# Side matmuls of all stages put one step behind the elementwise work that feeds them, in fewer and larger steps

## The chip, the cores and the metric

The kernel runs on one core of a Trainium2 chip. The metric is the device time of one execution in microseconds; the times quoted are medians of several runs.

## The reference, cut to what matters

Four layers act on 512 tokens of width 2048, all in float32. Each is a large projection in, a sequence mixer, gates, and a projection out that is added to the residual:

```python
def layer_ab(x, ...):            # 4 heads of gated linear attention (GLA), 8 of forgetting attention
    h = rms_norm(x, norm_g)
    g_q, g_k, g_v, g_lr, g_gate, f_q, f_k, f_v, f_f, f_gate = jnp.split(h @ w_in, split_idx, axis=-1)
    o = gla_chunked(...)                       # chunked recurrence, exp of cumulated decays
    o_fox = forgetting_attention(...)          # causal softmax(q k^T + decay) v
    return x + jnp.concatenate([o_gla, o_fox], axis=-1) @ w_out
def layer_c(x, ...):             # diagonal state-space model (S5), 128 groups of 16 channels
    u, gate = jnp.split(h @ w_in, 2, axis=-1)
    y = s5_ssm(u, ...)                         # x_t = Lbar x_{t-1} + Bbar u_t ; y = Re(C x) + D u
    z = jax.nn.gelu(y); z = z * jax.nn.sigmoid(z @ glu_w + glu_b)
    return x + (z * jax.nn.silu(gate)) @ w_out
def ssd_chunked(x, dt, A, B, C): # in layer D, run twice, beside a convolution of 31 taps and
    ...                                        # two pairs of heads of differential attention
    cb = jnp.einsum("bclgn,bcsgn->bcgls", Cc, Bc)
    y_diag = jnp.einsum("bcgls,bcgjls,bcsgjp->bclgjp", cb, decay_in, xdt)      # inside a chunk of 128
    states = jnp.einsum("bclgn,bcgjl,bclgjp->bcgjpn", Bc, decay_states, xdt)   # then a scan over chunks
    ...
    y_off = jnp.einsum("bclgn,bcgjpn,bcgjl->bclgjp", Cc, prev, jnp.exp(a_cs))  # from the chunks before
```

The order of the program is layer AB, layer C, layer D twice (D0, D1).

## The kernel before, in words

**Projections.** They carry most of the work of TensorE. A float32 product is made of three matmuls on numbers split in a high and a low part (`job_fm`, L244 to L246; `job_tm` and `job_tw` are the same for other layouts), 128x512 outputs in PSUM pool `pp` of 4 buffers. Weights come in units of 512 KB: SP issues the load to `raw` (4 buffers), ScalarE casts the high part (L224), VectorE or, for every fourth unit, GpSimd subtracts it for the low part (L227) into `whl` (3 buffers).

**Side work.** The mixers (GLA, attention, S5, SSD, convolution) and norms are Python generators in two lanes. After each quarter of a job, 24 projection matmuls, `mix()` adds a rate of the table `RATES` to a generator's account and runs one step (up to its next `yield`) for each whole unit; this makes a slot. There are 528 such slots in the program. `pump()` forces steps where a gate needs a result that isn't there yet. So a generator's side matmuls stand on TensorE's queue between projection matmuls, and TensorE works through its queue in order: a side matmul whose operand isn't ready holds up the projection behind it. The Tile framework's scheduler sets the final order from this emission. Side matmuls write to PSUM pool `ax` of 4 buffers; temporaries `t` come from a pool of 8.

```python
    def mix(self):
        for lane in self.lanes:
            if lane:
                m = lane[0]
                m[2] += m[1]
                while m[2] >= 1:
                    m[2] -= 1
                    ...next(m[0])...
```

**Names that follow.** In SSD (`ssd`, L1551), for each of 8 pairs of heads of a layer: the decay matrix is made by four subtract-and-clip instructions for each of the two heads (L1601), an exponential (L1603) and a product (L1604); psD, 8 matmuls of 128x64 tiles (L1617), is the part inside a chunk; psS (L1623) gives the states, which VectorE scans (multiply L1628, add L1630) into S; psO (L1639) multiplies S, one `yield` later. Each of them writes to `ax`. In S5 (`block`, L1189), 16 blocks: 16 matmuls of 64x64 tiles for V (L1202), rotations and scans on VectorE, GpSimd's products, then 4 full matmuls (L1234) and 16 of 64x64 tiles (L1241) for psY. In attention: rope's last sum (L1465), its transposes (L1469), the scores, the softmax, the transposes of p (L843), copied by ScalarE (L845), the products with v; differential attention scales p0 (L1512) before it adds p1. In the convolution branch a tap is L1660. L1565 transposes x for SSD; L190 and L415 sum and spread norms; L1083 and L1113 prepare S5's tables during layer AB; L1435 to L1439 and L855 to L871 are a setup block of tiny instructions for a layer's constants.

Of the kernel before, what the change touches and what calls it, by code (L numbers as in the profile page):

```python
# [9 lines left out]
F32 = mybir.dt.float32  # L10
# [8 lines left out]
D = 2048  # L19
S = 512  # L20
# [4 lines left out]
RATES = {"prep": 1.15, "gla": 2.0, "fox": 2.0, "s5": 4.0, "norm": 1.687, "ssd": 1.27,  # L25
         "att": 1.626, "cfm": 0.827, "dt": 1.0}
# [39 lines left out]
class Kern:  # L66
    def __init__(self, ctx, tc, I, O):
# [20 lines left out]
        self.unit_i = 0  # L88
        self.ahead = {}
# [31 lines left out]
    def small(self, shape, dt=F32, tag=None, bufs=None):  # L121
        tag = tag or f"s{shape[-1]}"
        return self.sm_p.tile(list(shape), dt, tag=tag, name=self.nm(tag),
                              bufs=bufs or (2 if tag in ("gst", "al4", "rm16", "rs16", "rt16", "selr") else 4))
# [70 lines left out]
    def bcast_rows(self, col):  # L195


        nc = self.nc
        ps = self.axp()
# [4 lines left out]
        for i, part in enumerate((hi.bitcast(F32), lo)):  # L204
# [3 lines left out]
            nc.tensor.matmul(ps, self.onesr, dg.rearrange("p c t -> p (c t)"), start=(i == 0), stop=(i == 1))  # L208
        return ps

# [20 lines left out]
    def job_fm(self, W, c0, X, evac, order=(0, 1, 2, 3)):  # L231
# [3 lines left out]
        for qi, kq in enumerate(order):  # L235
# [11 lines left out]
            self.mix()  # L247
        with self.tc.high_priority(offset=2000):
            for m in range(2):
                evac(m, ps[m])  # L250

    def job_tm(self, W, c0, X, evac, order=(0, 1, 2, 3)):
# [3 lines left out]
        for qi, kq in enumerate(order):  # L256
# [13 lines left out]
            self.mix()  # L270
        with self.tc.high_priority(offset=2000):
            for t in range(NC4):
                evac(t, ps[t // 2][:, t % 2, :])
# [18 lines left out]
    def job_tw(self, W, cols, X, evac, order=(0, 1, 2, 3)):  # L292
# [22 lines left out]
        p = parts(6) + parts(7)  # L315
        for t in range(NC4):
# [111 lines left out]
    def rs_pair(self):  # L428

        col = self.rs_columns(self.acc, D)  # L430
        rc = self.par.tile([128, 4], F32, tag="rscol", name=self.nm("rscol"))
        self.nc.vector.tensor_copy(out=rc, in_=col)
        ps = self.bcast_rows(col)
        row = self.par.tile([128, 512], F32, tag="rsrow", name=self.nm("rsrow"))
        self.nc.scalar.copy(out=row, in_=ps)
        return rc, row

# [96 lines left out]
    def layer_ab(self, resid, next_resid, order="to_uj", back=None):  # L534
# [46 lines left out]
        def small_cols():  # L581
# [15 lines left out]
            for q in (32, 64, 96):  # L597
                nc.vector.tensor_tensor(out=sm[0:24], in0=ps[q:q + 24, :], in1=sm[0:24], op=ALU.add)
            sc = self.xo([40, 512])
# [53 lines left out]
        def gla_head(sc, h):  # L653
# [3 lines left out]
            b = la.pop(h)  # L657
            yield
            if h < 3:
                la[h + 1] = gla_la(sc, h + 1)  # L660
                yield
            at = self.mx()
            ps = self.axp()
            for c in range(NC4):
# [4 lines left out]
                                    in1=self.ident.unsqueeze(1).to_broadcast([128, 4, 128]), op=ALU.mult)  # L669
            yield  # L670
            for li, s in enumerate((1, 2, 4, 8, 16, 32, 64)):
                nb = 512 // (2 * s)
                v3 = lambda t: t.rearrange("p (n e) -> p n e", e=2 * s)
                e = self.tmp(tag="t")
                r = v3(b)[:, :, s - 1:s].to_broadcast([128, nb, s])
                nc.vector.tensor_tensor(out=v3(e)[:, :, 0:s], in0=r, in1=v3(b)[:, :, 0:s], op=ALU.subtract)
                nc.vector.tensor_tensor(out=v3(e)[:, :, s:], in0=v3(b)[:, :, s:], in1=r, op=ALU.subtract)
                nc.scalar.activation(out=e, in_=e, func=AF.Exp, scale=1.0 / 16)
                G = e
                nc.vector.tensor_tensor(out=v3(G)[:, :, 0:s], in0=v3(e)[:, :, 0:s], in1=v3(k)[:, :, 0:s],  # L680
                                        op=ALU.mult)
                nc.vector.tensor_tensor(out=v3(G)[:, :, s:], in0=v3(e)[:, :, s:], in1=v3(q)[:, :, s:],
                                        op=ALU.mult)
                odd = lambda t: t.rearrange("p (n e) -> p n e", e=2 * s)[:, :, s:]
                ps = self.axp((128, 256))
                for c in range(NC4):
                    cs = slice(c * 128, (c + 1) * 128)
                    nc.tensor.matmul(ps[:, c * 64:(c + 1) * 64], G[:, cs], odd(G[:, cs]), start=True, stop=True)
                nc.vector.copy_predicated(
                    out=odd(at).rearrange("p (c n) e -> p c n e", c=4),  # L690
                    mask=odd(lev[:, li, :]).unsqueeze(1).to_broadcast([128, 4, 64 // s, s]),
                    data=ps.rearrange("p (c n e) -> p c n e", c=4, e=s))
                yield
            qe = self.tmp(tag="t")
            nc.scalar.activation(out=qe, in_=b, func=AF.Exp, scale=1.0 / 16)
            nc.vector.tensor_tensor(out=qe, in0=qe, in1=q, op=ALU.mult)
# [4 lines left out]
            nc.vector.tensor_tensor(out=ke, in0=ke, in1=k, op=ALU.mult)  # L701
            el = self.small([128, 4], tag="el")
            nc.scalar.activation(out=el, in_=c3(b)[:, :, 127], func=AF.Exp, scale=1.0 / 16)
            yield
# [5 lines left out]
            nc.scalar.copy(out=kt[:, 0:384], in_=ps[:, 0:384])  # L710
            yield
            po = [self.axp(), self.axp()]
            st = None
            for c in range(NC4):
                cs = slice(c * 128, (c + 1) * 128)
                for half in range(2):
                    nc.tensor.matmul(po[half][:, cs], v[c][:, half * 128:(half + 1) * 128], at[:, cs],
                                     start=True, stop=(c == 0))
                    if c > 0:
# [1123 lines left out]
```

## Time and profile before

| | |
|---|---|
| median of 3 runs | 3392.99 us (3390.59 to 3395.67) |
| profiled execution | 3397.99 us |
| its span | 3396.2 us |
| mean granted TensorE clock | 0.992 |
| VectorE, ScalarE, GpSimd busy | 63%, 34%, 30% of the span |

The profiled execution lies 5.0 us over the median. Of its 3397.99 us 1.8 lie outside the span.

### The profile page before, as it was taken

Reading aid. Unit: us, or ns where it says so; the run is one execution under the profiler, and the core shown is the slowest. Engines: PE = TensorE matmul, PEld = TensorE weight load, DVE = VectorE, ACT = ScalarE, POOL = GpSimd, SP = SyncE. Lnnn points to the kernel's source line nnn. Section 1 sums busy time; section 2 is a strip of 40 time slices with the busy share of each in tenths; the row PEclk is TensorE's granted clock in tenths of the full one; section 3 lists DMA queues with packets and bytes.
Section 4 is the critical chain, followed back from the end, with each engine's and each line's share of the span. In section 5 each row is a group of like instructions: output and inputs, shape, how many; then the busy total and the mean of one; then the engine's idle time right before and its main releaser. Section 6 shows DMA issues by size and latency. Waiting matters only on the chain.

```text
span 3396.2 us, 46458 instructions
## 1 busy us (share of the span) xinstructions
PE 3310.2 (97%) x17238; PEld 2710.6 (80%) x17238; DVE 2155.2 (63%) x4409; ACT 1160.3 (34%) x1915; POOL 1007.8 (30%) x993
## 2 busy tenths in 40 slices
PE   8999999999999999999999999988999999998999
PEld 6887887877887777888887878867788787886887
DVE  7765785668347787424257586897526468699632
ACT  4223333334232222323233333324324343323421
POOL 3122414433523333122332121147321212125720
PEclk9999999999999999999999999999999999999999
DMA  6323333344545664434334232333343323233243
GB/s 208 90 71 116 104 106 99 108 122 152 186 129 174 197 209 156 144 120 128 120 108 131 85 87 81 105 104 86 115 139 112 92 83 87 81 112 106 81 134 115
DMA packets 389713, 406.12 MB, mean 120 GB/s; under 512 B 53296, under 2 KB 334774, under 8 KB 389486
## 3 DMA queue, kind: packets, MB, share of 16 engines
q1 hardware_dynamic: 389486, 403.15, 39.3%
q8 instruction: 136, 2.23, 0.3%
q14 instruction: 91, 0.75, 0.1%
HBM read 348.45 MB, written 54.59 MB: 119 GB/s over the span
## 4 chain that ended last, share of the span: by engine, by line
PE 61%; DVE 15%; DMA 3%; issue 2%; POOL 2%; SPq 1%; ACT 1%; DVEq 0%; POOLq 0%; ACTq 0%
PE pp L244 15%; PE pp L246 15%; PE pp L245 15%; PE pp L306 3%; PE pp L305 3%; PE pp L304 3%; DVE mx L1660 2%; DVE whl L227 2%; DVE t L1601 1%; DMA t<-acs 1%; DVE xo L1545 1%; POOL mx L1664 1%; POOL t L1224 1%; DVE ev L517 1%; PE pp L269 1%
## 5 line engine op out<-in xcount | busy, mean ns | idle before, releaser
L246 PE MATMUL pp<-hl,whl 128*128 128x512 f32 x3328 | 1310.5, 394 | 12.1 <-DVE whl L227 9.1
L244 PE MATMUL pp<-hl,whl 128*128 128x512 f32 x3328 | 1314.9, 396 | 3.5 <-ACT hl L328 3.4
L245 PE MATMUL pp<-hl,whl 128*128 128x512 f32 x3328 | 1313.9, 395 | 1.0 <-DVE hl L329 1.0
L224 ACT CAST whl<-raw 128x1024 fp32r<-128x1024 f32 x440 | 461.8, 1050 | 966.3 <-PE pp L246 703.1
L227 DVE TENSOR_TENSOR whl<-raw,whl 128x1024 fp32r<-128x1024 f32 x330 | 428.6, 1299 | 516.7 <-ACT whl L224 510.2
L246 PEld LDWEIGHTS pp<-hl,whl 128*128 128x128 f32 x3328 | 629.4, 189 | 145.9 <-DVE whl L227 10.4
L244 PEld LDWEIGHTS pp<-hl,whl 128*128 128x128 f32 x3328 | 629.5, 189 | 137.5 <-issue 5.8
L245 PEld LDWEIGHTS pp<-hl,whl 128*128 128x128 f32 x3328 | 629.4, 189 | 129.6 <-issue 1.9
L227 POOL TENSOR_TENSOR whl<-raw,whl 128x1024 fp32r<-128x1024 f32 x110 | 277.1, 2519 | 861.8 <-ACT whl L224 776.3
L305 PE MATMUL pp<-whl,hl 128*128 128x512 f32 x704 | 275.6, 392 | 0.0
L306 PE MATMUL pp<-whl,hl 128*128 128x512 f32 x704 | 275.5, 392 | 0.0
L304 PE MATMUL pp<-whl,hl 128*128 128x512 f32 x704 | 273.3, 393 | 0.0
L392 POOL TENSOR_TENSOR t<-t,t 128x512 f32<-128x512 f32 x75 | 111.5, 1498 | 280.0 <-ACT t L385 277.9
L287 ACT CAST whl<-raw 128x1024 fp32r<-128x1024 f32 x88 | 92.3, 1052 | 248.0 <-PE pp L306 187.8
L288 DVE TENSOR_TENSOR whl<-raw,whl 128x1024 fp32r<-128x1024 f32 x66 | 87.1, 1320 | 128.2 <-ACT whl L287 128.1
L1660 DVE SCALAR_TENSOR_TENSOR mx<-xo,col,mx 128x511 f32<-128x511 f32 (+19 forms) x180 | 160.4, 904 | 0.8
L304 PEld LDWEIGHTS pp<-whl,hl 128*128 128x128 f32 x704 | 132.7, 188 | 28.5 <-issue 0.9
L306 PEld LDWEIGHTS pp<-whl,hl 128*128 128x128 f32 x704 | 132.6, 188 | 28.2 <-issue 0.9
L305 PEld LDWEIGHTS pp<-whl,hl 128*128 128x128 f32 x704 | 132.7, 188 | 27.0
L288 POOL TENSOR_TENSOR whl<-raw,whl 128x1024 fp32r<-128x1024 f32 x22 | 53.8, 2446 | 257.9 <-ACT whl L287 245.2
L269 PE MATMUL pp<-whl,hl 128*128 128x256 f32 x384 | 108.2, 285 | 1.0 <-DVE hl L329 1.0
L267 PE MATMUL pp<-whl,hl 128*128 128x256 f32 x384 | 108.6, 285 | 0.5 <-ACT hl L328 0.5
(443 smaller groups left out, 4088.1 us busy)
## 6 DMA issues: line engine op xcount, KB each, us to landing
raw<-w_in SPq DMA_DIRECT2D x160, 512.0 KB
raw<-ab_w_in SPq DMA_DIRECT2D x112, 512.0 KB
raw<-c_w_in SPq DMA_DIRECT2D x64, 512.0 KB
raw<-w_out SPq DMA_DIRECT2D x64, 512.0 KB
raw<-ab_w_out SPq DMA_DIRECT2D x32, 512.0 KB
raw<-glu_w SPq DMA_DIRECT2D x32, 512.0 KB
raw<-c_w_out SPq DMA_DIRECT2D x32, 512.0 KB
raw<-w_in SPq DMA_DIRECT2D x64, 256.0 KB
```

The source lines that it names most:

```text
L224: nc.scalar.copy(out=hl[:, 0, :, :n], in_=raw[:, :, :n])
L227: eng.tensor_tensor(out=hl[:, 1, :, :n], in0=raw[:, :, :n], in1=hl[:, 0, :, :n].bitcast(F32), op=ALU.subtract)
L244: nc.tensor.matmul(ps[m], wh, x[:, 0, :], start=first, stop=False)
L245: nc.tensor.matmul(ps[m], wh, x[:, 1, :], start=False, stop=False)
L246: nc.tensor.matmul(ps[m], wl, x[:, 0, :], start=False, stop=last)
L269: nc.tensor.matmul(o, xl, hl[:, 0, j, :], start=False, stop=last, skip_group_check=True)
L288: (nc.gpsimd if pool else nc.vector).tensor_tensor(out=hl[:, 1], in0=raw, in1=hl[:, 0].bitcast(F32), op=ALU.subtract)
L304: nc.tensor.matmul(ps[t], x[:, 0, ts], hl[:, 0, j, :], start=first and i == 0, stop=False)
L305: nc.tensor.matmul(ps[t], x[:, 0, ts], hl[:, 1, j, :], start=False, stop=False)
L306: nc.tensor.matmul(ps[t], x[:, 1, ts], hl[:, 0, j, :], start=False, stop=last and i == n - 1)
L392: nc.gpsimd.tensor_tensor(out=a, in0=a, in1=sq, op=ALU.add)
L1660: STT(out=Y[i][:, d:], in0=u, scalar=k, in1=Y[i][:, d:], op0=ALU.mult, op1=ALU.add)
```

## The change

It changes when side work is emitted, not what is computed. In every mixer the matmuls of a step now come one step after the elementwise work that makes their operands, and several such groups share a step; the rates are lowered to match, so that generators finish at about the same slots as before (S5's blocks at slot 206 for 196, S5's preparation at 136 for 117, GLA's pairs at 37 and 69 for 35 and 63, the second attention pair of D0 at 322 in both). Steps of a generator fall: GLA's pair 37 to 19, forgetting attention's pair 19 to 11, differential attention's pair 34 to 22, SSD's half 19 to 16, S5 16 blocks of 12 to 139 in all.

Further: forgetting and differential attention are pipelined, with the scores of block n, the transposes of n-1 and the products of n-2 in one step. S5's psY matmuls of block b (64x64 and full) and V of block b+1 are issued together. GLA makes two levels in a step. Rope transposes all its tiles after all its sums. Norms (`rs_pair`, layer D's norms, `ssd_norm`) become generators of two steps, with a flag `rs_ready` that evacuations wait for. ScalarE takes over from VectorE: L1601 (as 128 `Relu`), the convolutions' first taps (L1543 and the 31-tap one) and the layer norm's last scaling; p0's scaling (L1512) falls away, its factor moved into the square and the norm behind it. The number of TensorE matmuls (15670), of DMAs (1406) and the arithmetic of the matmuls stay.

```diff
-RATES = {"prep": 1.15, "gla": 2.0, "fox": 2.0, "s5": 4.0, "norm": 1.687, "ssd": 1.27,
-         "att": 1.626, "cfm": 0.827, "dt": 1.0}
+RATES = {"prep": 0.95, "gla": 0.95, "fox": 1.0, "s5": 2.25, "norm": 1.687, "ssd": 1.05,
+         "att": 1.05, "cfm": 0.827, "dt": 1.0}
...
+            for n in range(len(items) + 2):
+                if n >= 2:
+                    h, qb = items[n - 2]
...
+                    for s in range(qb + 1):
+                        nc.tensor.matmul(po[h][:, qs], vt["f", h][s], t[:, s, :], start=(s == 0), stop=(s == qb))
...
+                if 1 <= n <= len(items):
+                    pt[n - 1] = self.transpose_p(pr.pop(n - 1), items[n - 1][1])
+                if n < len(items):
+                    pr[n] = fox_scores(*items[n], lfhl)
+                yield
...
+                psY = [self.ax.tile([128, 2, 128], F32, tag="ax", name=self.nm("psY")) for _ in range(2)]
                 for h in range(2):
...
+                                nc.tensor.matmul(psY[g][half[i], h, :], w[half[g], 4 + 2 * r + h, half[i]],
+                                                 xs[i][half[g], h, r, :], start=(h + r == 0), stop=False,
+                                                 skip_group_check=True)
+                for g in range(2):
+                    for h in range(2):
+                        nc.tensor.matmul(psY[g][:, h, :], w[:, 8 + 2 * g + h, :], ut[:, g, h, :], start=False,
+                                         stop=True, skip_group_check=True)
+                if b + 1 in us:
+                    cur = inputs(b + 1)
                 yield
...
+            def off_diagonal(i, S, ea):
+                psO = self.axp((128, 384))
+                for c in range(3):
+                    cs = slice(c * 128, (c + 1) * 128)
+                    nc.tensor.matmul(psO[:, cs], S[:, cs], C[:, (c + 1) * 128:(c + 2) * 128], start=True,
+                                     stop=True)
...
-                        TS(out=rb[hh][:, cs], in0=rb[hh][:, cs], scalar1=dac[:, c, 32 + h:33 + h], scalar2=0.0,
-                           op0=ALU.subtract, op1=ALU.min)
-                    nc.scalar.activation(out=rb[hh], in_=rb[hh], func=AF.Exp)
+                        nc.scalar.activation(out=rb[hh][:, cs], in_=rb[hh][:, cs], func=AF.Relu, scale=-1.0,
+                                             bias=dac[:, c, 32 + h:33 + h])
+                    nc.scalar.activation(out=rb[hh], in_=rb[hh], func=AF.Exp, scale=-1.0)
...
+                if prev is not None:
+                    off_diagonal(*prev)
                 psD = self.axp()
```

What this does to the order is seen best on TensorE's queue. In D0's SSD, before, psO's three matmuls of one pair stand one by one between projection matmuls, here the first of them (S is `t_19054`):

```order
L246 MATMUL pp_19526<-hl_16095,whl_19601 128x512
L244 MATMUL pp_19525<-hl_16131,whl_19601 128x512
L1639 MATMUL ax_19076<-xo_17621,t_19054 128x128
L245 MATMUL pp_19525<-hl_16131,whl_19601 128x512
L246 MATMUL pp_19525<-hl_16131,whl_19601 128x512
L244 MATMUL pp_19526<-hl_16131,whl_19601 128x512
```

The same place of the changed kernel (L254 to L256 are the projection, L1748 psO, L1783 psD, L1789 psS, L1738 the transposes of the next x):

```order
L256 MATMUL pp_19161<-hl_15968,whl_19164 128x512
L1748 MATMUL ax_19191<-xo_17610,t_19073 128x128 x3
L1783 MATMUL ax_19197<-t_19059,t_19071 64x128
L1783 MATMUL ax_19197<-t_19060,t_19071 64x128
L1783 MATMUL ax_19197<-t_19059,t_19071 64x128
L1783 MATMUL ax_19197<-t_19060,t_19071 64x128
L1783 MATMUL ax_19197<-t_19059,t_19071 64x128
L1783 MATMUL ax_19197<-t_19060,t_19071 64x128
L1783 MATMUL ax_19197<-t_19059,t_19071 64x128
L1783 MATMUL ax_19197<-t_19060,t_19071 64x128
L1789 MATMUL ax_19206<-t_19150,dx_18734 128x128 x3
L1738 MATMUL ax_19218<-ident,xo_18037 128x128 x4
L254 MATMUL pp_19160<-hl_16009,whl_19234 128x512
```

All 18 stand in one run: psO of the pair before, then psD and psS of this pair. Over the program, between the end of the work on S and a psO matmul (counted from the psS matmul that S comes from) there were 9 projection matmuls at least, mostly 16 to 24; now 24 is the least, which 10 of the 48 psO matmuls have, and 30 of the 48 have 72. For psD the least count is 24 as before, but 96 of 128 rows now have 72. For rope's transposes the least goes from 77 to 120, for psY's from 36 to 56. The p transposes of differential attention had as few as 0 and have 16 at least.

In layer C, TensorE's queue before, where two of S5's 16 psY matmuls stand alone, with the other 14 ten rows on:

```order
L245 MATMUL pp_10728<-hl_9831,whl_10849 128x512
L246 MATMUL pp_10728<-hl_9831,whl_10849 128x512
L1241 MATMUL psY_10841<-t_10782,s5w_10758 64x128
L1241 MATMUL psY_10842<-t_10782,s5w_10758 64x128
L244 MATMUL pp_10727<-hl_9845,whl_10915 128x512
L245 MATMUL pp_10727<-hl_9845,whl_10915 128x512
```

And after, the end of the 16 psY matmuls of a block (L1345), its full ones (L1350) and the first V matmuls of the next block (L1284):

```order
L1345 MATMUL psY_10999<-t_10930,s5w_10782 64x128
L1345 MATMUL psY_10999<-t_10933,s5w_10782 64x128
L1350 MATMUL psY_10998<-mx_10616,s5w_10782 128x128 x2
L1350 MATMUL psY_10999<-mx_10616,s5w_10782 128x128 x2
L1284 MATMUL psV_11024<-mx_10854,s5w_11020 64x128 x2
L1284 MATMUL psV_11025<-mx_10854,s5w_11020 64x128 x2
```

Over the program the runs of side matmuls between projection matmuls go from 399 to 307, those of 64x64 tiles from 70 to 53, those of psD's tiles from 30 to 18.

VectorE's queue in D0's SSD, before: the clips (L1601), the states' scan (L1628, L1630) and the weights' subtraction (L227) in between the taps.

```order
L1601 TENSOR_SCALAR t_19062<-t_19062,dac 128x128 x4
L1660 SCALAR_TENSOR_TENSOR mx_20051<-xo_18971,col_15890,mx_20051 128x508
L1628 TENSOR_TENSOR t_19054<-t_19054,el 128x128
L1601 TENSOR_SCALAR t_19063<-t_19063,dac 128x128 x4
L1660 SCALAR_TENSOR_TENSOR mx_20372<-xo_19355,col_15890,mx_20372 128x508
L1660 SCALAR_TENSOR_TENSOR mx_20051<-xo_18971,col_15890,mx_20051 128x507
L1604 TENSOR_TENSOR t_19062<-t_19062,dx_18724 128x512
L1630 TENSOR_TENSOR t_19054<-t_19054,ax_19050 128x128
L227 TENSOR_TENSOR whl_19754<-raw_19752,whl_19754 128x1024
```

After, the scan (L1796, L1798) with the product of the decays (L1768) and the taps (L1816); no clips are left on this engine.

```order
L1816 SCALAR_TENSOR_TENSOR mx_19597<-xo_18967,col_15818,mx_19597 128x505
L1798 TENSOR_TENSOR t_19225<-t_19225,ax_19206 128x128
L1768 TENSOR_TENSOR t_19211<-t_19211,dx_18728 128x512
L1816 SCALAR_TENSOR_TENSOR mx_19597<-xo_18967,col_15818,mx_19597 128x504
L1796 TENSOR_TENSOR t_19225<-t_19225,el 128x128
L1768 TENSOR_TENSOR t_19212<-t_19212,dx_18728 128x512
L1816 SCALAR_TENSOR_TENSOR mx_19597<-xo_18967,col_15818,mx_19597 128x503
```

VectorE has 4253 instructions for 4411, ScalarE 1955 for 1789. The setup block of D1, which stood late in D0 with one weights' subtraction in its middle, stands there in one piece ahead of the next subtraction.

## Rows read from the trace of the kernel before

**Rows 1.** The page's part 1: engine, busy us, share of the span, instructions.

```profile
PE 3310.2 (97%) x17238; PEld 2710.6 (80%) x17238; DVE 2155.2 (63%) x4409; ACT 1160.3 (34%) x1915; POOL 1007.8 (30%) x993
```

**Rows 2.** The waits of TensorE: us in total, times, longest.

```profile
PE ax L1639 <- DVE t L1630: 14.6, 8, 4.0
PE pp L246 <- DVE whl L227: 9.1, 3, 6.6
PE ax L1469 <- DVE xo L1465: 8.3, 8, 3.2
PE psY L1241 <- DVE t L1227: 8.0, 7, 2.1
PE ax L153 <- DMA t<-ab_norm_g: 7.3, 1, 7.3
PE ax L1617 <- DVE t L1604: 6.9, 8, 1.9
PE ax L843 <- DVE t L834: 4.4, 2, 2.8
...
PE ax L1565 <- DVE xo L1632: 2.2, 2, 1.1
...
PE pp L267 <- ACT hl L328: 0.5, 1, 0.5
...
PE ax L190 <- POOL t L1687: 0.2, 1, 0.2
```

**Rows 3.** TensorE's timeline in layer C: start us, us of one, instruction, count.

```profile
1109.02 0.39 PE L245 MATMUL pp<-hl,whl 128*128 128x512 f32 x1
1109.25 0.39 PE L246 MATMUL pp<-hl,whl 128*128 128x512 f32 x1
1109.57 0.43 PE L1241 MATMUL psY<-t,s5w 64*64 64x128 f32 x4
...
1110.27 0.39 PE L245 MATMUL pp<-hl,whl 128*128 128x512 f32 x1
...
1112.12 0.40 PE L244 MATMUL pp<-hl,whl 128*128 128x512 f32 x1
1112.45 1.09 PE L1241 MATMUL psY<-t,s5w 64*64 64x128 f32 x28
...
1113.80 0.39 PE L246 MATMUL pp<-hl,whl 128*128 128x512 f32 x1
```

**Rows 4.** Windows at half clock: stretch, us, PE busy (count), clock, DMA, GB/s.

```profile
518.54:528.78 10.24, 6.58 (x17) 0.50 0.17 46
...
1836.09:1839.50 3.41, 3.41 (x11) 0.50 0.10 14
...
sum 54.61, PE 47.82; mean PE 5.31
```

**Rows 5.** Timeline of D0's SSD: the scan's multiply on VectorE, the waiting psO.

```profile
2260.10 1.36 DVE L1628 TENSOR_TENSOR t<-t,el 128x128 f32<-128x128 f32 x1
...
2264.66 0.49 PE L1639 MATMUL ax<-xo,t 128*128 128x128 f32 x2 [3.85 <-DVE t L1630]
```

**Rows 6.** SSD's clips on VectorE (timeline, then group); an activation on ScalarE (group).

```profile
2286.97 4.58 DVE L1601 TENSOR_SCALAR t<-t,dac 128x128 f32<-128x128 f32 x4
...
2291.67 0.86 DVE L1601 TENSOR_SCALAR t<-t,dac 128x128 f32<-128x128 f32 x4
...
L1601 DVE TENSOR_SCALAR t<-t,dac 128x128 f32<-128x128 f32 x128 | 38.4, 361 | 9.3 <-DMA t<-acs 9.3
...
L1525 ACT ACTIVATE t<-ax 128x128 f32<-128x128 f32 x32 | 8.9, 277 | 48.3 <-PE ax L1523 48.3
```

**Rows 7.** Window of D0's SSD: busy us of PE, PEld, DVE, ACT, POOL.

```profile
2130.00:2420.00 290.00, 265.08 (x1296) 213.91 (x1294) 252.88 (x422) 107.11 (x161) 126.72 (x82) 0.98 0.33 97
```

**Rows 8.** VectorE's timeline: the setup block's start, and a weights' subtraction inside it.

```profile
2326.60 0.66 DVE L1435 TENSOR_TENSOR dr<-dr,dr 128x64 f32<-128x64 f32 x1 [5.19 <-DMA dr<-att_lambda_k]
...
2340.16 2.26 DVE L227 TENSOR_TENSOR whl<-raw,whl 128x1024 fp32r<-128x1024 f32 x1
```

More of the change, by code (lines that the diff above doesn't have):

```diff
@@ new lines, in gla_tail @@
+        def gla_tail(h, po, q, k):
+            sq = [self.tmp(tag="t") for _ in range(2)]
+            out = []
+            for half in range(2):
+                nc.scalar.activation(out=sq[half], in_=po[half], func=AF.Square)
+                o = (q, k)[half]
+                nc.scalar.activation(out=o, in_=po[half], func=AF.Copy,
+                                     scale=hg[:, 2 * h + half:2 * h + half + 1])
+                out.append(o)
+            nc.gpsimd.tensor_tensor(out=sq[0], in0=sq[0], in1=sq[1], op=ALU.add)
+            yield
+            parts = self.bcast_parts(self.rs_columns(sq[0], 256))
+            yield
+            ps = self.bcast_sum(parts)
+            for half in range(2):
+                nc.vector.tensor_tensor(out=out[half], in0=out[half], in1=ps, op=ALU.mult)
+                O[2 * h + half] = out[half]
+            yield
@@ L669, in gla_head @@
                                     in1=self.ident.unsqueeze(1).to_broadcast([128, 4, 128]), op=ALU.mult)
+            lv = [gla_level(b, q, k, s) for s in (1, 2)]
+            nxt()
             yield
[L671 to L692, printed above, removed]
+            for two in ((4, 8), (16, 32)):
+                new = [gla_level(b, q, k, s) for s in two]
+                for x in lv:
+                    gla_scores(at, x)
+                lv = new
+                nxt()
                 yield
-            qe = self.tmp(tag="t")
-            nc.scalar.activation(out=qe, in_=b, func=AF.Exp, scale=1.0 / 16)
-            nc.vector.tensor_tensor(out=qe, in0=qe, in1=q, op=ALU.mult)
+            new = [gla_level(b, q, k, 64)]
             ke = self.tmp(tag="t")
@@ new lines, in inter, with state @@
+                    nc.tensor.matmul(po[half][:, cs(c)], st[:, hs[half]], qe[:, cs(c)], start=False, stop=True,
+                                     skip_group_check=True)
+            def state(c, st, ps):
+                ns = self.small([128, 256], tag="gst")
+                if c == 0:
+                    nc.scalar.copy(out=ns, in_=ps)
+                else:
+                    nc.vector.scalar_tensor_tensor(out=ns, in0=st, scalar=el[:, c:c + 1], in1=ps, op0=ALU.mult,
+                                                   op1=ALU.add)
+                return ns
@@ L1114, in s5_blocks @@
                                         self.ident)
+            b3 = pr([128, 2, 4, 4, 16])
+            for i in range(2):
+                nc.scalar.copy(out=b3[:, i], in_=bb[i][:, :, 3].unsqueeze(2).to_broadcast([128, 4, 4, 16]))
             vt = self.tmp([128, 4, 128])
@@ L1118, in s5_blocks @@
             yield
-            b3 = pr([128, 2, 4, 4, 16])
-            for i in range(2):
-                nc.scalar.copy(out=b3[:, i], in_=bb[i][:, :, 3].unsqueeze(2).to_broadcast([128, 4, 4, 16]))
             psK = [self.axp((128, 2, 64)) for _ in range(2)]
```

539 lines of the change are left out of this document (314 added, 225 removed).

## The prediction

> **What bounds the kernel now.** I read the page's engine line first: TensorE is busy for 97% of the span, VectorE for 63% [rows 1]. So the span is TensorE's own work plus what holds it up, and a change that leaves the number of matmuls alone can give three things only: waits, clock, and matmuls that cost less where they stand. The list of TensorE's waits gives the first. Its 24 rows sum to 81.1 us, from 14.6 down to 0.2 [rows 2]. Of these 7.3 are the start (L153) and 18.0 are waits of projection matmuls for weights or inputs, six rows from 9.1 to 0.5. The other 17 rows are side matmuls: 55.8 us. Five rows of them, L1639, L1469, L1241, L1617 and L843, hold 42.2; the other twelve, from 2.2 (L1565) down, hold 13.6. The reader is to see the releaser: in all five it is the last VectorE instruction of a short chain that was emitted one step before, and the waits are short and many (8 times 1.8 us for L1639). The timeline shows one: VectorE began the multiply of the scan at 2260.10 and psO, on the queue already, went ahead at 2264.66 after a wait of 3.85 us [rows 5].
>
> The second is the granted clock. In a window view of the stretches at clock 0.50, which is 1.2 GHz instead of 2.4, nine stretches sum to 54.61 us with 47.82 us of TensorE work in them [rows 4]. Five of the nine come behind waits of the five rows above: the one at 518.54, after L843's, with 6.58 us of work, and four of one 3.41 us slice each, behind L1469 (1836.09), L1639 (2266.17) and two like them in D1.
>
> The third is seen in TensorE's timeline of layer C. Projection matmuls start 0.23 us apart (1109.02, 1109.25). With 4 matmuls of 64x64 tiles between them, two pitches take from 1109.25 to 1110.27, 1.02 us; with 28, from 1112.12 to 1113.80, 1.68 us [rows 3]. So 24 more of them cost 0.66 us, 27.5 ns each; 4 cost 0.11 by that, and 1.02 - 0.45 - 0.11 leaves **0.46 us for a run of such tiles, whatever its length**.
>
> **The change, part by part.**
>
> *Waits.* A slot of 24 projection matmuls takes 24 times 0.227, 5.45 us. What a side matmul needs has now at least that much TensorE work before it. psO: the scan ran from 2260.10 to 2264.6, 4.5 us, with the longest taps between its parts [rows 5]; with 24 matmuls at least, 72 in most groups, the wait of 14.6 us falls to about 3, left for the 10 matmuls that have only one slot. L1469: from 77 matmuls at least to 120, longest wait 3.2 us, less than the 9.8 us added; 0 left. L1241: from 36 to 56, 4.5 us more, longest wait 2.1; 0 left. L1617: the least stays at 24, but three quarters of the rows go to 72; 2 of 6.9 left. L843: from 0 to 16, 3.6 us more, longest 2.8; 0 left. Together 42.2 becomes 5. Of the twelve small rows some are moved (L1083, L1113) and some aren't (L1534 gets no more cover); half, 7. **Waits: -44.** The weights' waits and the start stay: no load moves in number, and their queue on SP is as it was.
>
> *Clock.* At half clock, work of b us would take b/2. If the five waits go, the stretches behind them do: 6.58/2 + 4 times 3.41/2 = 10. **Clock: -10.** Between 0 (the throttle answers something else) and 47.82/2 = 24 (all nine go); the rows show a stretch behind each of these waits, so I take the five.
>
> *Runs of other tiles.* 64x64 runs fall by 17, 15 of them in S5 where psY, its full matmuls and the next V become one burst; psD's runs fall by 12. At 0.46 us each, 15 give 6.8 and 12 give 5.5. No row shows the price for psD's 128x64 tiles alone; below it is 0, above 0.46; I take the upper, since the tile shape changes there as well. **Runs: -12**, between -7 and -12. Full matmuls merged into one run gain nothing that I can see, so the other 63 runs that disappear count zero.
>
> *VectorE to ScalarE.* 128 clips (38.4 us) go to ScalarE, 277 ns for an activation of such a tile from PSUM, so 35 us there [rows 6]. The first taps and the layer norm's scaling follow them. In D0's SSD VectorE is busy for 253 of 290 us, ScalarE for 107 [rows 7], so ScalarE has 183 us to cover its share of the new work, and TensorE waits for neither by itself: nothing in the sum beyond the waits above. It is what makes the shorter chains likely: four clips took 0.86 us alone and 4.58 beside GpSimd's work, on the queue in front of the scan [rows 6]. If the cover were gone, the price would be that of psD behind a later exponential, at most the 6.9 of L1617 again. The Trainium skill (Perfetto Trace Analysis, Optimizing Scalar/DVE Operations) says that an operation which both engines can do is faster on VectorE where a performance mode applies, and that moving it pays if VectorE is saturated. By its first half ScalarE's clips would come later than VectorE's did and psD would wait its 6.9 us as before: 3338 for 3333. The rows bear out the second half (253 of 290 us busy) and speak against the first (277 ns against a mean of 361).
>
> *What is added.* Norms wait for a flag, which forces a step where they aren't ready: cost nothing with the slot before as cover, and 5.45 us of chain per layer without. p0's products hold a buffer of `ax` over several steps, and temporaries live one step longer (8 buffers). D1's setup block now stands in one piece before a weights' subtraction: it started at 2326.60 and let one subtraction through at 2340.16, and the projection still waited 6.6 us [rows 2, 8]; I add 2. For buffers, 4, since none of the rows shows a wait on `ax` itself being free; bounds 0 and what the third rival gives. **Added: +6.**
>
> Sum: -44 - 10 - 12 + 6 = -60. The profiled execution took 3398.0 us, so 3338; the median lies 5.0 below it: **3333 us**, 1.8% faster.
>
> **The rivals.**
>
> *Waits are moved, not removed.* VectorE stays the busiest helper, its queue still holds the taps and the weights' subtractions, and 10 of 48 psO matmuls have just 5.45 us of cover for a scan that took 4.5 with a copy and a wait on psS before it. With several groups in one run, the latest operand of all holds the run up. Against it: 72 matmuls of cover, 16 us, for most. If half the waits come back (22), the clock gives back nothing and runs 7, the sum is -22 - 7 + 6 = -23: 3375 profiled, 3370 median.
>
> *No change.* The scheduler could put the moved matmuls back where their operands allow, or the weights' supply could take up what the side work frees. The order shows the moves as written, and the projections wait only 18.0 us for weights and inputs [rows 2]. Then the sum is the difference of small terms: 3388 to 3398 for the median.
>
> *PSUM becomes the bound, slower.* `ax` has 4 buffers. A pipelined step of differential attention holds the sum of products, two score tiles and a tile for the transposes, all four, and S5's preparation or a norm in the other lane wants a fifth. Then the next side matmul waits for ScalarE or VectorE to empty one, and the projection behind it waits too. The price is a helper's instruction, 0.28 us for a 128x128 tile [rows 6], times one or two per step. There are 170 such steps (4 pairs of forgetting attention by 11, 2 of GLA by 19, 4 of differential attention by 22). It decides from (60 + 7)/170 = 0.39 us a step; at 0.28 it would cost 48 (3381), at two instructions 0.55 and 94, so 3427 us. The Trainium skill (Perfetto Trace Analysis, Identifying Performance Opportunities) holds that a gap that repeats for a stretch on the engine that should be saturated can mean too few SBUF or PSUM buffers. No such gap stands in the trace of before; longer lives of buffers are where it would appear.
>
> **How the numbers follow.** The forecast has a chance of 0.66, moved waits 0.17, no change 0.07, PSUM 0.10. Low end: all 55.8 of side waits, the clock of all nine stretches (24) and 12 for runs, nothing added: 3398 - 92 - 5 = 3301, say 3300. High end: the first rival and half a dozen us of its uncertainty above 3370, so 3378. Outside lie the PSUM rival, no change and little else, some 0.19. The forecast's own range is 3312 to 3352. A measurement of this kernel can tell 0.2%, 6.8 us: faster 0.83, same 0.07, slower 0.10.
>
> **What would show it.** In TensorE's waits after: L1748 (psO) at 3 us or so, L1588 (rope) and L1345 (psY) gone, L1783 (psD) at 2, weights about 18 to 20 as before. In windows: no half clock after 520, 1836, 2266, 3088 and 3116. In layer C's timeline: one burst a block, and layer C some 15 us shorter (8.0 of waits, 6.8 of runs). In D0's SSD VectorE's busy time well below 253 and ScalarE's above 107. The prediction is wrong if new rows appear whose releaser is a ScalarE copy of an `ax` tile (the third rival), if psO's or psD's row stays above 7 us (the first), or if TensorE's busy time doesn't fall with its runs, in which case the run price was that of something else.

## The result, and the profile after

The changed kernel takes 3354.09 us (median of 4 runs, 3344.65 to 3362.33) beside 3394.33 in the same rounds: ratio 0.988, interval 0.985 to 0.991. It is faster by 1.2%, 40 us where 61 were forecast from a median of 3394. Its runs spread over 18 us, those of before over 8; the profiled execution is the fastest of the eight runs that were made of it in all (median 3356.2), and its span is 53.3 us shorter than that of before.

The page of the changed kernel, part 1, with the columns of [rows 1]:

```profile
PE 3276.3 (98%) x17238; PEld 2709.9 (81%) x17238; DVE 2139.1 (64%) x4251; ACT 1224.3 (37%) x2081; POOL 1011.1 (30%) x993
```

TensorE's own busy time fell by 33.9 us. Its waits, to be read against [rows 2], fell by 18.7, from 81.1 to 62.4:

```profile
PE ax L1748 <- DVE t L1798: 26.0, 8, 6.7
PE ax L154 <- DMA t<-ab_norm_g: 7.1, 1, 7.1
PE ax L785 <- DVE gst L793: 5.8, 1, 5.8
PE ax L1192 <- POOL pr L1002: 3.9, 2, 3.4
PE pp L255 <- DVE hl L342: 3.7, 1, 3.7
...
PE ax L1588 <- DVE xo L1580: 2.7, 2, 2.4
PE psY L1345 <- DVE t L1336: 2.4, 2, 2.2
...
PE pp L256 <- DVE whl L237: 1.1, 2, 0.8
...
PE pp L254 <- ACT hl L341: 0.5, 1, 0.5
```

Rope, psY, psD and the p transposes went nearly as forecast: 8.3 to 2.7, 8.0 to 2.4, and the rows of psD (6.9) and of the p transposes (4.4) are gone. The row that was to fall most, psO's 14.6, rose to 26.0, and one of 5.8 is new: GLA's products on the state (L785). The spreading of norms (L215, L190 before) waits 3.6 for 0.2. S5's preparation (L1192, L1113 before) waits 3.9 for about 2.7. The projections' own waits, which I left as they were, fell from 18.0 to 5.3.

To see where the time went, I took the start of the same projection matmul (they are the same 13248 in both) near each layer's end, from the two traces:

| us | before | after | difference |
|---|---|---|---|
| AB, to projection matmul 3940 | 1004.3 | 1001.6 | -2.7 |
| C, to 7200 | 822.6 | 804.1 | -18.5 |
| D0, to 10250 | 822.4 | 806.0 | -16.3 |
| D1, to the last | 742.7 | 726.7 | -16.0 |

Layer AB, with the most rewritten code (GLA and forgetting attention), gave almost nothing; each of the other three some 16 to 19.

Half clock came back in part. Windows of the changed kernel at clock 0.50, columns of [rows 4] (a last slice at the program's end left out):

```profile
412.91:419.74 6.83, 4.16 (x13) 0.50 0.30 80
...
2225.39:2232.21 6.82, 3.94 (x24) 0.50 0.27 79
2252.69:2262.93 10.24, 6.53 (x30) 0.50 0.49 138
...
sum 47.78, PE 33.64; mean PE 4.81
```

Work at half clock went from 47.82 to 33.64 us; half of the difference, 7 us, is what the clock gave by the forecast's own rule. The stretches of 520 and 1836 are gone as forecast; those behind psO are still there, longer.

### The profile page after: what moved, and what is told of

Read it like the earlier page. It is cut to its first block, busy times and chain, and to the rows that moved or that the text cites. A ratio compares the mean times of both kernels' runs of the same rounds, so it can differ in the third digit from the quotient of the medians.

```text
span 3342.9 us, 46470 instructions
## 1 busy us (share of the span) xinstructions
PE 3276.3 (98%) x17238; PEld 2709.9 (81%) x17238; DVE 2139.1 (64%) x4251; ACT 1224.3 (37%) x2081; POOL 1011.1 (30%) x993
## 4 chain that ended last, share of the span: by engine, by line
PE 75%; DVE 10%; POOL 2%; issue 1%; DMA 1%; ACT 0%; SPq 0%; POOLq 0%; DVEq 0%; ACTq 0%
PE pp L254 18%; PE pp L255 18%; PE pp L256 18%; PE pp L316 3%; PE pp L317 3%; PE pp L318 3%; DVE mx L1816 3%; DVE whl L237 1%; PE pp L278 1%; PE pp L280 1%; PE pp L279 1%; DVE xo L1697 1%; PE ax L1652 1%; PE psY L1350 0%; PE psY L1345 0%
## 5 line engine op out<-in xcount | busy, mean ns | idle before, releaser
L254 PE MATMUL pp<-hl,whl 128*128 128x512 f32 x3328 | 1311.1, 395 | 0.6 <-ACT hl L341 0.5
L255 PE MATMUL pp<-hl,whl 128*128 128x512 f32 x3328 | 1305.4, 392 | 3.7 <-DVE hl L342 3.7
L256 PE MATMUL pp<-hl,whl 128*128 128x512 f32 x3328 | 1304.0, 392 | 1.1 <-DVE whl L237 1.1
L254 PEld LDWEIGHTS pp<-hl,whl 128*128 128x128 f32 x3328 | 627.7, 189 | 131.4 <-ACT t L1358 1.7
L256 PEld LDWEIGHTS pp<-hl,whl 128*128 128x128 f32 x3328 | 626.9, 188 | 131.8 <-DVE whl L237 2.4
L255 PEld LDWEIGHTS pp<-hl,whl 128*128 128x128 f32 x3328 | 627.5, 189 | 131.0 <-DVE hl L342 4.1
L1816 DVE SCALAR_TENSOR_TENSOR mx<-xo,col,mx 128x511 f32<-128x511 f32 (+19 forms) x180 | 173.6, 994 | 4.7 <-ACT mx L1814 3.8
```

The source lines that it names most:

```text
L254: nc.tensor.matmul(ps[m], wh, x[:, 0, :], start=first, stop=False)
L255: nc.tensor.matmul(ps[m], wh, x[:, 1, :], start=False, stop=False)
L256: nc.tensor.matmul(ps[m], wl, x[:, 0, :], start=False, stop=last)
L1816: STT(out=Y[i][:, d:], in0=u, scalar=k, in1=Y[i][:, d:], op0=ALU.mult, op1=ALU.add)
```

## Experiments

The times beside each are medians, with the ratio to the kernel before in the same rounds.

**SSD's mixer alone, and differential attention's alone.**

The first has the function `ssd` of the change and

```diff
-RATES = {"prep": 1.15, "gla": 2.0, "fox": 2.0, "s5": 4.0, "norm": 1.687, "ssd": 1.27,
+RATES = {"prep": 1.15, "gla": 2.0, "fox": 2.0, "s5": 4.0, "norm": 1.687, "ssd": 1.05,
```

> The kernel before with SSD's mixer of the change and its rate, nothing else (clips on ScalarE, psO one step later in one run with psD and psS). Theory (the gain in D is this mixer's, and its psO waits come with it): D0 and D1 together 25 to 33 us shorter, 3362 to 3369 us, psO's waits near 26 us for 14.6. Rival (the D gain comes from the other edits, the norms, attention, first taps): under 12 us, 3382 or more, psO near 15.

The second has `att_rope` to `att_pair` of the change and

```diff
-         "att": 1.626, "cfm": 0.827, "dt": 1.0}
+         "att": 1.05, "cfm": 0.827, "dt": 1.0}
```

> The kernel before with differential attention's mixer of the change and its rate, nothing else. SSD's mixer alone gave 11.4 us of the 32 that D lost. Theory (most of the rest is attention: fewer runs, rope's transposes and p's transposes no longer waiting): D0 and D1 together 10 to 16 us shorter, 3380 to 3385, rope's wait 2 to 3 us for 8.3, runs in D 150 to 160 for 200. Rival (the rest is VectorE's relief by the other edits): 3392 or more.

SSD's alone: 3383.73, ratio 0.9961 (0.9947 to 0.9975), 14.5 us shorter in D by the trace; its psO waits are 11.1, not 26. Attention's alone: 3386.13, ratio 0.9966 (0.9954 to 0.9978), 13.3 us shorter in D. Neither theory holds as written: SSD's time is the rival's (3382 or more), with a psO row that neither named; attention's gain in D is the theory's, but its reasons aren't, as the rows below show. The two sum to 27.8 of the 32.3 that D lost, so the gain is shared. And psO's long row comes with the other mixer: with attention's edit alone, SSD's code untouched, it reads

```profile
PE ax L1675 <- DVE t L1666: 28.4, 13, 4.8
...
PE ax L1472 <- DVE xo L1464: 7.8, 6, 2.2
...
PE pp L246 <- DVE whl L227: 3.8, 3, 1.6
```

(L1675 is psO, L1472 rope, in that kernel's numbering). Rope's wait hardly moved, and runs in D went from 200 to 191 only. In both kernels it is the projections' waits for weights and inputs that fell, from 18.0 us to under 9 in each.

**Layer C alone.** The function `layer_c` of the change, with its one generator for all blocks:

```diff
-                for m in range(2):
-                    self.add_mixer(block(2 * c + m), RATES["s5"])
...
+            self.add_mixer(blocks(), RATES["s5"])
```

> The kernel before with layer C's mixer of the change and its rate, nothing else. In the two traces layer C became 18.6 us shorter: 7.2 of waits and 11.4 by 45 fewer runs of side matmuls, about 0.25 us for a run. Theory (the gain of layer C is made in layer C, by runs and waits): 3394 - 18 = 3376 us, a wait row of psY of 2.4 us for 8.0, runs in layer C 25 for 70. Rival (layer C gains only since other stages hand over earlier): under 8 us, 3386 or more.

3379.79, ratio 0.9951 (0.9938 to 0.9963); layer C 19.1 us shorter in the trace up to matmul 7200, runs 25 for 70, psY's wait under 2 us. The theory holds: what layer C gains is made there. By the medians of the same rounds layer C alone gives 15.4 us, SSD alone 11.4 and attention alone 11.1, together 37.9 of the 40 (each known to some 4 us).

**What a run costs.** First by cutting S5's burst:

```diff
+                yield
                 for g in range(2):
...
+                yield
                 if b + 1 in us:
```

(The rate of S5 goes from 2.25 to 2.77.)

> The changed kernel with S5's burst cut in three steps (psY's 64x64 tiles, its full ones, V of the next block) at a rate raised to match; the matmuls and their tiles are the same and in the same order. Theory (each interruption of the projection's stream costs, 0.25 us, whatever the tiles): 32 more runs, +8 us, 3362. Rival (the change of tile shape costs, 0.46 us, as I forecast): the burst had both 64x64 groups already, so no change, 3354, within 3 us.

3365.55, ratio 0.9909 (0.9896 to 0.9923). The scheduler joined most of the pieces again, 11 runs more instead of 32, while psY's waits grew from 2.4 to 7.8 us and its profile holds a loss in layer AB that is told of below. So it says nothing on the price. A direct measure was better, side matmuls that only cost time:

```diff
+        kind = self.probe_n // 4 % 5
+        n = {0: 0, 1: 8 * (j == 3), 2: 2, 3: 8 * (j == 3), 4: 2}[kind]
```

> The changed kernel with side matmuls that nothing reads added in layer C's last 28 slots of job_fm, in rotation: none, 8 full ones in one run, 8 full ones in four runs of 2, 8 of 64x64 tiles in one run, 8 of those in four runs. Read from the trace, slot by slot. Theory (an interruption costs about 0.25 us whatever the tiles): four runs cost 0.75 us a slot more than one run, for both kinds. Rival (the tile shape costs 0.46 us and full ones nothing, as I forecast): 0 for the full ones, 1.4 us for the 64x64 tiles.

TensorE's timeline of that kernel (L271 to L273 are the projection, L252 full side matmuls, L255 those of 64x64 tiles; one matmul shows as 2):

```profile
1427.06 0.40 PE L273 MATMUL pp<-hl,whl 128*128 128x512 f32 x1
1427.30 1.95 PE L252 MATMUL ax<-ident 128*128 128x128 f32 x16
...
1429.32 0.40 PE L272 MATMUL pp<-hl,whl 128*128 128x512 f32 x1
...
1430.24 0.40 PE L273 MATMUL pp<-hl,whl 128*128 128x512 f32 x1
1430.48 0.61 PE L252 MATMUL ax<-ident 128*128 128x128 f32 x4
...
1431.16 0.40 PE L272 MATMUL pp<-hl,whl 128*128 128x512 f32 x1
...
1441.68 0.39 PE L273 MATMUL pp<-hl,whl 128*128 128x512 f32 x1
1442.00 0.67 PE L255 MATMUL ax<-ident 64*64 64x128 f32 x16
...
1442.94 0.40 PE L272 MATMUL pp<-hl,whl 128*128 128x512 f32 x1
...
1443.86 0.39 PE L273 MATMUL pp<-hl,whl 128*128 128x512 f32 x1
1444.18 0.43 PE L255 MATMUL ax<-ident 64*64 64x128 f32 x4
...
1444.88 0.39 PE L272 MATMUL pp<-hl,whl 128*128 128x512 f32 x1
```

From L273 to the second matmul behind, less two pitches of 0.227: full, 1.81 us for x16 and 0.47 for x4, so 112 ns for each and 0.02 for the run; 64x64, 0.81 and 0.57, so 20 ns for each and 0.49 for the run. Summed until the projection is back at its pitch, four runs instead of one cost 0.10 us more for full matmuls (0.03 for each further run) and 1.57 for the small tiles (0.52). The theory of one price for every run falls; the forecast's price of 0.46 for a change of tiles and next to nothing for full ones stands. The Trainium skill (TensorEngine Tiling (Array Packing), Key Properties) has it that a change of the tiling mode drains TensorE; 0.49 beside 0.02 us agree.

**VectorE's clips back, the rest of the change kept.**

```diff
-                        nc.scalar.activation(out=rb[hh][:, cs], in_=rb[hh][:, cs], func=AF.Relu, scale=-1.0,
-                                             bias=dac[:, c, 32 + h:33 + h])
+                        TS(out=rb[hh][:, cs], in0=rb[hh][:, cs], scalar1=dac[:, c, 32 + h:33 + h], scalar2=0.0,
+                           op0=ALU.subtract, op1=ALU.min)
```

> The changed kernel with SSD's clips back on VectorE (L1601 of before), all else kept. Theory (relief of VectorE is what lowered the weights' waits in D from 16.4 to 4.5 us): weights' waits in D back above 10, psO and psD waits longer, 3354 + 10 = 3364 us. Rival (the order alone did it, the move is worth nothing): 3354 within 4 us, weights' waits at 5.

3362.33, ratio 0.9891 (0.9873 to 0.9909), against 3357.87 and 0.9883 (0.9867 to 0.9899) for the changed kernel in the same rounds: times alone don't tell them apart. In the one trace of each, D takes 8.9 us longer, psD waits 9.0 us again, and D0's waits of the projection are 8.5 us for 4.5, under the theory's 10; psO waits 19.0 us, less than the 26.0 of the changed kernel. So the move to ScalarE looks worth some 9 us in D, which the medians, 4.5 us apart with runs that spread over 21 and 10, don't confirm.

**Why psO waits.** The scan with half the depth:

```diff
-                    TT(out=h2(S[:, cs]), in0=h2(S[:, pv]),
-                       in1=el[:, c, 2 * i:2 * i + 2].unsqueeze(2).to_broadcast([128, 2, 64]), op=ALU.mult)
-                    TT(out=S[:, cs], in0=S[:, cs], in1=psS[:, cs], op=ALU.add)
+                    for hh in range(2):
+                        a = c * 128 + hh * 64
+                        STT(out=S[:, a:a + 64], in0=S[:, a - 128:a - 64], scalar=el[:, c, 2 * i + hh:2 * i + hh + 1],
+                            in1=psS[:, a:a + 64], op0=ALU.mult, op1=ALU.add)
```

> The changed kernel with SSD's scan of states made of two independent multiply-adds per chunk (64 columns each) in place of a multiply and an add that depend on each other: the same count of VectorE instructions, half the depth, and on VectorE's queue 3 rows from first to last in place of up to 13. Theory (psO waits since the scan's four instructions stand between taps and weight subtractions on VectorE's queue): psO's 26.0 us fall below 12, with the half-clock stretches behind them, 3354 - 17 = 3337 us. Rival (psO stands too near to psS on TensorE, whatever VectorE's order): psO stays above 20 us and the time within 5 us of 3354.

3344.86, ratio 0.9851 (0.9834 to 0.9868). Its waits:

```profile
PE ax L1783 <- DVE t L1768: 12.2, 4, 5.9
PE ax L1748 <- DVE t L1797: 10.8, 4, 4.6
```

psO fell below 12 as the theory has it, so its wait hangs on the scan's way through VectorE's queue; but psD, in the same run of matmuls, now waits 12.2 us for its decay product, so only 3.0 of the 26.0 us are won there, and the half clock in D's SSD stays (17.1 and 13.7 us in D0 and D1, as in the changed kernel). Profile against profile it is 6.4 us shorter (3336.5 for 3342.9), 5.0 of them in D; 17 were expected.

**The new wait in GLA.** The preparation of S5 (`s5_blocks`) as before, whose loads stand one `yield` later:

```diff
-            for i, nme in enumerate(("s5_b_re", "s5_b_im")):
...
             yield
+            for i, nme in enumerate(("s5_b_re", "s5_b_im")):
...
```

> The changed kernel with the mixer that prepares S5's tables as it was before (its loads in the step that uses them), all else kept. Theory (the one new wait of GLA's products on the state, 5.8 us at 416 with half clock behind it, comes from VectorE standing 9.9 us on the load of these tables): that wait goes, 3354 - 8 = 3346 us. Rival (the wait is GLA's own merged steps): it stays at 5 us or more, 3354 within 4.

In the changed kernel VectorE stands idle for this load up to 412.84 (L999), and GLA's wait of 5.8 us ends at 415.6:

```profile
412.84 0.23 DVE L999 TENSOR_TENSOR pr<-pr,s5cfi 128x64 f32<-128x64 f32 x1 [9.94 <-DMA pr<-s_b_re]
```

3345.29, ratio 0.9849 (0.9833 to 0.9864). L785's row is gone with the stretch at 412, VectorE's 9.94 us are 0.75, and AB is 5.9 us shorter in the trace than the changed kernel's. The theory holds for this wait: VectorE stood on a load that was emitted earlier, and what was queued behind it came late. The whole span is only 2.2 us shorter, since layer C is 2.9 us longer; the median's 11 us below 3356.2 is more than this trace explains.

**D1's setup block.**

```diff
+            if l == 1:
+                return tabs, self.nlam
```

> The kernel before, where D1 takes the lambda of D0 instead of its own: it leaves out the part of D1's setup block that computes it, 24 VectorE instructions. Theory (the 6.6 us wait of the projection for a weights' subtraction late in D0 comes from this block on VectorE's queue): that wait and the half-clock stretch at 2341 go, 3394 - 9 = 3385 us. Rival (VectorE is behind there anyway, by clips and taps): a wait of 4 us or more stays, 3394 within 4.

3395.87, ratio 0.9999 (0.9990 to 1.0007). The theory falls: a wait of 3.9 us stays where 6.6 were, with 3.4 us of half clock behind it for 6.8, and the time is the same. The part that was left out can account for 2.7 us of that wait at most.

**The spread.** The changed kernel again, then with one subtraction moved:

```diff
-        eng = nc.gpsimd if self.unit_i % 4 == 3 else nc.vector
+        eng = nc.gpsimd if self.unit_i % 4 == 3 and self.unit_i != 15 else nc.vector
```

> The changed kernel once more, for its spread: its runs so far lie 18 us apart (3345 to 3362), those of before 8. The same program of layer AB lost 9.5 us in one profile, where a weights' subtraction on GpSimd at 144 us took 14.71 us for 2.57, the projection waited 4.6 us and half clock followed. Theory (this subtraction is sometimes shut out, and makes the spread): two groups of times some 10 us apart, 3345 to 3362, median near 3352. Rival (drift of the chip): before spreads as far in the same rounds.

> The changed kernel with one of its 440 weights' subtractions, the sixteenth, on VectorE instead of GpSimd: the one at 144 us, which took 14.71 us in three profiles and 2.57 in one. Theory (GpSimd is shut out by VectorE's GLA instructions there in some executions, which costs 9.6 us each time): the wait at 159 never comes, the median falls by 4 to 8 us to about 3350, the spread by half. Rival (the wait comes from late weights, whichever engine subtracts): 3355 within 3 us, spread as before.

The first: 3357.87 (3352.44 to 3361.99), no two groups, but its profile holds the slow subtraction. GpSimd's and VectorE's timeline there:

```profile
144.46 14.71 POOL L237 TENSOR_TENSOR whl<-raw,whl 128x1024 fp32r<-128x1024 f32 x1 [21.59 <-ACT whl L234]
...
144.36 0.42 DVE L691 TENSOR_TENSOR t<-mx 128x256 f32<-128x256 f32 x1
144.69 0.42 DVE L690 TENSOR_TENSOR t<-mx 128x256 f32<-128x256 f32 x1
...
159.22 0.80 PE L256 MATMUL pp<-hl,whl 128*128 128x512 f32 x1 [4.64 <-POOL whl L237]
```

and the same place of the fastest execution:

```profile
144.32 2.57 POOL L237 TENSOR_TENSOR whl<-raw,whl 128x1024 fp32r<-128x1024 f32 x1 [21.59 <-ACT whl L234]
...
144.55 2.62 DVE L690 TENSOR_TENSOR t<-mx 128x256 f32<-128x256 f32 x1
```

In the one GpSimd got in first and one VectorE instruction of 0.42 us took 2.62; in the other VectorE's instructions of GLA's levels followed each other without a gap until 157, GpSimd came out after 14.71 us, the projection waited 4.64 and 10.24 us at half clock followed: 9.7 us by projection matmul 960. With that one subtraction on VectorE, 3345.52 (3343.55 to 3348.64), ratio 0.9851 (0.9838 to 0.9863): 11 us less than the median of the eight runs of the changed kernel, and a spread of 5 for 18. This fits the theory, with more won than the 4 to 8 us expected. But four runs don't settle how much of the spread is this race: with S5's preparation as before and the subtraction still on GpSimd, the median was 3345.29 and the spread 8. A second loss, of some 8 us, stands in the same profile, in layer C at 1172, behind a late load of S5's rotation table (VectorE idle 9.57 us for 4.76). Over seven traces TensorE's wait at that place grows with this idle time: 1.2 us at most up to 6.8 us idle, then 4.5, 5.0 and 6.1 at 7.9, 8.4 and 9.6. The trace with 7.9 is that of the next kernel, with the sixteenth subtraction on VectorE; so this loss doesn't follow from the first. No run removed it.

**All three mends.**

The diffs of the fused scan, of S5's preparation and of the moved subtraction together.

> The changed kernel with the fused scan of SSD, S5's preparation as before, and the sixteenth subtraction on VectorE. Theory (the three losses are separate): -9, -9 and -5 from 3355, so 3332 us, 3327 to 3338. Rival (they share a cause, VectorE's queue, and what one frees another takes): 3340 or more.

3336.22 (3331.20 to 3343.63), ratio 0.9824 (0.9810 to 0.9838), 1.8% below before and 20.0 us below 3356.2, inside the theory's range. The medians don't show that the losses are separate, though: singly they lie 11.3, 10.9 and 10.7 us below 3356.2, 33 in all. The medians of four runs hold a varying share of losses that come in some executions. In the traces, against the fastest execution of the changed kernel, AB is 4.6 us shorter (5.9 with the preparation alone) and D 4.1 (5.0 with the scan alone), so these two gains stand side by side; layer C is 7.8 us longer, most of it by the second loss, in what was the slowest of the four runs.

## Why the prediction was right, and where it was wrong

The direction and the range (3300 to 3378) held; the gain was 40 us where 61 were forecast. The 3354 us lie 2 outside the forecast's own range (3312 to 3352), between its 3333 and the first rival's 3370, and psO's row stayed above 7 us, which was the sign set for that rival. That the profiled executions came close to the sum (53.3 us of 60) is in part luck: the one after is the fastest of eight, and the terms missed in both directions. By the steps of the sum, on these two executions:

- *Waits, -44: they gave 18.7.* psO rose by 11.4 where a fall of 11.6 stood; the other four rows fell from 27.6 us to 5.1, nearly as forecast; the small rows, of which half was to go, rose from 13.6 to 18.9, with those of GLA, the norms and S5's preparation; the projections' fell by 12.7, and the start by 0.2.
- *The step that failed is psO's:* "with 24 matmuls at least, 72 in most groups, the wait of 14.6 us falls to about 3". Both sides of this comparison were wrong. The scan of 4.5 us, from 2260.10 to 2264.6, is its first multiply and add alone. In the kernel before, the chain of that pair, from psS (L1623) by way of the scan's last add to the last psO matmul, reads

```profile
2251.18 0.94 PE L1623 MATMUL ax<-t,dx 128*128 128x128 f32 x6
...
2268.23 0.28 DVE L1628 TENSOR_TENSOR t<-t,el 128x128 f32<-128x128 f32 x1
...
2272.66 0.27 DVE L1630 TENSOR_TENSOR t<-t,ax 128x128 f32<-128x128 f32 x1
...
2272.98 0.49 PE L1639 MATMUL ax<-xo,t 128*128 128x128 f32 x2
```

The whole scan takes 12.8 us there, and the chain from the end of psS 20.8. The same for a pair of the changed kernel, with ScalarE's copy, the scan's two pairs and the matmul that waited:

```profile
2203.69 0.94 PE L1789 MATMUL ax<-t,dx 128*128 128x128 f32 x6
...
2211.33 0.25 ACT L1793 COPY t<-ax 128x128 f32<-128x128 f32 x1
...
2218.07 0.77 DVE L1796 TENSOR_TENSOR t<-t,el 128x128 f32<-128x128 f32 x1
2218.77 2.96 DVE L1816 SCALAR_TENSOR_TENSOR mx<-xo,col,mx 128x494 f32<-128x494 f32 x2
2221.65 0.28 DVE L1798 TENSOR_TENSOR t<-t,ax 128x128 f32<-128x128 f32 x1
...
2225.32 0.28 DVE L1796 TENSOR_TENSOR t<-t,el 128x128 f32<-128x128 f32 x1
2225.53 1.22 DVE L237 TENSOR_TENSOR whl<-raw,whl 128x1024 fp32r<-128x1024 f32 x1
2226.66 1.36 DVE L1816 SCALAR_TENSOR_TENSOR mx<-xo,col,mx 128x492 f32<-128x492 f32 x2
2227.94 0.28 DVE L1798 TENSOR_TENSOR t<-t,ax 128x128 f32<-128x128 f32 x1
2228.28 0.80 PE L1748 MATMUL ax<-xo,t 128*128 128x128 f32 x2 [5.81 <-DVE t L1798]
```

Four short instructions take from 2218 to 2228, since each stands in VectorE's queue behind taps and a weights' subtraction, and the copy ran 16.9 us before the wait ended. The chain from the end of psS is 23.6 us. Nor did TensorE's lead grow where it was needed. Before, the scheduler had spread psO's three matmuls out: "mostly 16 to 24" projection matmuls is right for 26 of the 48, but the third of a pair, which needs the whole scan, stood 62 and 63 behind psS at the two pairs of D0 that waited longest. So these had 17.0 and 21.3 us of lead against chains of 20.8 and 24.4, and the waits there, 3.9 and 3.2, are the difference; after, all three stand at 72, with 17.5 and 17.3 us against 23.6 and 23.9. All 26 us of waits are at groups with 72; the 10 matmuls with one slot of lead, 24 to 27, for which the 3 us were left, don't wait at all. This is what the first rival said of psO, though not at the 10 matmuls that it named; "the latest operand of all holds the run up" is what the fused scan showed, when psO's wait fell and psD's came. VectorE was full in the 30 us ahead of such a wait in both kernels (before, then after; window: PE, PEld, DVE, ACT, POOL busy), so its load alone doesn't explain why the wait grew:

```profile
2234.66:2264.66 30.00, 24.94 (x129) 19.96 (x129) 29.79 (x47) 9.32 (x14) 11.95 (x8) 1.00 0.37 116
...
2198.28:2228.28 30.00, 23.39 (x123) 19.20 (x121) 30.00 (x36) 10.91 (x21) 17.69 (x10) 0.95 0.27 81
```

Why attention's edit alone makes psO's row long stays open.
- *"No load moves in number", so the projections' waits stay: wrong, by 12.7 us in our favour.* The two mixers alone each lowered them; in the trace with the clips back D0's were 8.5 for 4.5. Why each lowers them stays open. The setup block, priced at +2, is at most a small part (without its lambda the time was the same), and no row shows the +4 for buffers.
- *VectorE to ScalarE:* the reading "277 ns against a mean of 361" was of another activation, from PSUM. The clips themselves took 388 ns on ScalarE, 49.7 us for the 35 forecast, and more than on VectorE. psD's row went all the same. In D0 VectorE's busy time fell from 253 to 230 us of 290 and ScalarE's rose from 107 to 122, as forecast.
- *Clock, -10: 7.* The two stretches behind L843 and L1469 went, those behind psO stayed with their waits. L843's two waits, at 520.6 and 525.9, are forgetting attention's in layer AB, though the forecast counted the lead of differential attention; that this row went as forecast is luck in part.
- *Runs, -12: too small.* TensorE's busy time less the clock fell by 27. The price held: the 4 and 28 of [rows 3] are records, two to a matmul, but the 0.46 us for a run came out at 0.49. For 17 runs of 64x64 tiles that is 8.3. Runs of psD's tiles alone are in the trace of before, of 2 and 14 records, with 0.56 and 1.23 us beyond two pitches, so 0.45 for a run and 5.4 for 12. The other 63, put at zero, give 2 at 0.03 each. That is 16; some 11 us stay open. Runs of 64x128 tiles fell too, from 40 to 32, and no run here shows their price.
- *The third rival* left no trace: no wait on a ScalarE copy of an `ax` tile appears among the 14 rows. The rule of the Trainium skill on repeating gaps and too few buffers (Perfetto Trace Analysis, Identifying Performance Opportunities) had no case here.
- *Not foreseen:* the new wait behind a load moved earlier, which is in the profiled execution too, and losses that come in some executions only. The profiled execution's gain (53) is 13 us above the median's (40), since the one after lies 9.4 us below its median and the one before 3.7 above.

## What to carry to other kernels

Putting a consumer later on the engine that bounds helped where the lead grew, as for rope (77 to 120 projection matmuls) and psY (36 to 56). Take lead and chain from the trace, for the same consumer: the whole chain, from the matmul it starts at, with all that stands between its instructions on the helper's queue, and the lead that the scheduler already gives the consumer. Where the helper's queue is full, a shorter chain on it helped (psO's row 26.0 to 10.8), but the next operand of the same run was then the late one. Give a change's median several runs: a share of the loss here came in some executions only, and the profiled one didn't hold it.

## What was not expected of the hardware

One GpSimd subtraction of 128x1024 took 2.57 us or 14.71 in executions of the same code (14.71 in three of the seven traces with the changed kernel's GLA in which GpSimd has it), as it seems by which engine came first. The Trainium skill (SBUF — State Buffer, Who interferes with whom) has it that a VectorE instruction with two inputs in SBUF contends with a GpSimd instruction that reads SBUF, and that the port pair which they share is an exclusive lock. The 2.62 us of a VectorE instruction of 0.42 agree. The 14.71 go beyond it: GpSimd did not get in between the VectorE instructions that followed one another from 144.03 on, most of them every 0.33 us, until VectorE's row ended at 157.
